# Odd mixer of a two-layer hybrid trunk on one core: the place of the column tiles among the S5 states, and the engine of each convolution chunk

## The chip, the cores and the metric

The kernel runs on one core of a Trainium2 chip. A core has four engines that compute, each with its own queue of instructions: TensorE (PE in the profile; PEld is its loading of weights), VectorE (DVE), ScalarE (ACT) and GpSimd (POOL). SyncE (SP) issues the DMA transfers of this kernel. The metric is the device time of one execution in microseconds; lower is better. Three runs of the kernel before took 1369.16, 1368.41 and 1371.1 us.

## The reference, cut to what matters

The trunk has two layers; each is a mixer and a gated ConvFFN with residual adds. The change lies in the mixer of the second (odd) layer, with a sequence of 512, a model width of 1024 and 512 channels in each of the two branches:

```python
def odd_mixer(h, w_in, conf_dw_w, conf_dw_b, conf_ln_g, conf_ln_b, s5_a_re, s5_a_im,
              s5_b_re, s5_b_im, s5_c_re, s5_c_im, s5_d, s5_log_step, s5_glu_w, w_out):
    proj = h @ w_in
    ca, cg, u = split_cols(proj, [CONF_DIM, CONF_DIM, S5_DIM])
    c = ca * jax.nn.sigmoid(cg)
    c = causal_dwconv(c, conf_dw_w, conf_dw_b)
    c = jax.nn.silu(layer_norm(c, conf_ln_g, conf_ln_b)).astype(F32)
    s = jax.nn.gelu(s5_ssm(u, s5_a_re, s5_a_im, s5_b_re, s5_b_im, s5_c_re, s5_c_im, s5_d, s5_log_step))
    s = s * jax.nn.sigmoid(s @ s5_glu_w.astype(F32))
    mix = jnp.concatenate([c, s], axis=-1).astype(h.dtype)
    return mix @ w_out
```

The depthwise convolution has 31 taps. The S5 part is a complex diagonal recurrence for 32 groups of 16 channels with 64 states each.

## The kernel before, in words

Activations lie transposed: the channels on the 128 partitions, the 512 steps along the free dimension, eight tiles for the model width. A product with a weight is made in three matmuls of 128x512 (lines L100, L101, L102), since weights and activations are split into a high part `hi` and a rest `lo` in a shorter format: hi x hi, hi x lo and lo x hi. A weight tile is loaded by SP into `wraw` (four buffers), cast to `whi` by ACT (L90) and its rest `wlo` made by DVE (L91); `whi` and `wlo` have three buffers each. One column tile of an input product is 8 x 3 = 24 matmuls.

The odd mixer works in four column tiles of 128 channels for each of three products. `glu_in(i)` makes the two products `pca` and `pcg` of the convolution's tile i, multiplies both by the norm's row `R` on DVE, and gates one with the sigmoid of the other. `s5_state(q)` makes the product `pu` of S5 tile q, its multiple `uf` (DVE), regroups it by transposes on PE with copies on ACT between them (`pu2`, `u2`, `puT`, `us`), makes the drive `pS` on PE, and then runs the states on DVE: rotations, two scans (L928, L929) and more rotations into `sst`. `s5_y` makes the outputs `pY` from `us` and `sst` with the matrices `toep` and `w2`, `s5_split` transposes them back (`pyT`), applies GELU and splits the result into `sh` and `slo` for the gate product `pgl`. The output product `po` comes last, and the layer norm of the convolution's result lies beside it. In the profile's names the copies of `u2` show as `u` and the tiles `pu2` as `pu`.

The four chunks of the convolution are made on three engines. For the chunks in `PECONV` (2 and 3) the gated tile is written twice, the second time shifted by a step (`cx`; DVE writes one half, ACT copies the other), and `conv_pe` makes 32 matmuls of 64 output partitions with diagonal weights `kd`, two taps in each. Chunk 0 is in `POOLTAPS`: its 30 taps behind the first run on GpSimd, two instructions each (L858, L859). Chunk 1 has its 30 taps on DVE (L869).

The order of instructions on each engine is fixed when the program is built. The order in the source gives the priority; a `with issue_after(x)` adds that the instructions in it stand behind x on the same engine, with no wait in it. Most tiles of 128x512 come from one pool of 56 slots, and a DMA that fills a slot waits until its last reader is done. PSUM has two sets of four buffers, `pp` for products and `ps` for the rest.

Of the kernel before, what the change touches and what calls it, by code (L numbers as in the profile page):

```python
# [13 lines left out]
ALU = mybir.AluOpType  # L14

P = 128
T = 512
# [6 lines left out]
RH = 4  # L24
SH = 16
NPAIR = SH // 2
POOLTAPS = {0: range(1, 31)}
PECONV = (2, 3)
WV0 = (0, 1, 3, 6)
PACK0 = (("g_mix0", KC),)  # L30
PACK1 = (("ident", P), ("tri", P), ("cw", 48), ("cb", 12), ("dtb", SH), ("alog", SH), ("dsk", NPAIR),
# [5 lines left out]
class Trunk:  # L37
# [774 lines left out]
    def odd(self, st):  # L812
        nc = self.nc
# [4 lines left out]
        mm = nc.tensor.matmul  # L818
        V = nc.vector.tensor_tensor
        cin, cv = [None] * 4, [None] * 4  # L820
        def glu_in(i):
            pa = self.pp("pca")
            self.proj(pa, ins["wca"][i], xs)
            pg = self.pp("pcg")
            self.proj(pg, ins["wcg"][i], xs)
            if "R" not in st:
                self.norm_end(st)
            R = st["R"]
            if i in PECONV:
                a = self.tmp("ca")  # L830
            else:
                a = self.tp.tile([P, T], F32, name="cp", tag="cp", bufs=2) if i in POOLTAPS else self.slot("ca")
            b = self.tmp("cg")
            V(a, pa, R, op=ALU.mult)
            V(b, pg, R, op=ALU.mult)
            nc.scalar.activation(b, b, AF.Sigmoid)
            if i in PECONV:

                x2 = [self.slot("cx") for _ in range(2)]
                for g in range(2):  # L840
                    own, oth = slice(64 * g, 64 * g + 64), slice(64 - 64 * g, 128 - 64 * g)
                    V(x2[g][own], a[own], b[own], op=ALU.mult)
                    nc.vector.memset(x2[g][oth, 0:1], 0.0)
                    nc.scalar.copy(x2[g][oth, 1:], x2[g][own, :T - 1])
                cin[i] = x2
                return
            V(a, a, b, op=ALU.mult)
            cin[i] = a
            o = self.slot(f"cv{i}")
            nc.scalar.activation(o, a, AF.Identity, scale=kw[:, i, 30:31], bias=kb[:, i:i + 1])  # L850
            cv[i] = o
            pa = o
            if i in POOLTAPS and len(POOLTAPS[i]) < 30:
                pa = self.slot("cvp")
                nc.gpsimd.memset(pa, 0.0)
            for s in POOLTAPS.get(i, ()):
                t = self.tp.tile([P, T], F32, name="prod", tag="prod", bufs=1)
                nc.gpsimd.tensor_scalar(t, a, kw[:, i, 30 - s:31 - s], 1.0, op0=ALU.mult, op1=ALU.mult)  # L858
                nc.gpsimd.tensor_tensor(pa[:, s:], pa[:, s:], t[:, :T - s], op=ALU.add)  # L859
            cvp[i] = pa  # L860
# [11 lines left out]
        def conv_loads(i):  # L872
            for h in range(4):
                t = self.slot("kd")
                ld(t, ins["kd"][PECONV.index(i), :, h * T:(h + 1) * T])
                kd.setdefault(i, []).append(t)

        def conv_pe(i):

            p = self.ps("pcv")  # L880
            for j in range(16):
                s = 2 * j
                for g in range(2):
                    w = kd[i][j // 4][:, (j % 4) * P + 64 * g:(j % 4) * P + 64 * g + 64]
                    mm(p[64 * g:64 * g + 64, s:], lhsT=w, rhs=cin[i][g][:, :T - s], start=j == 0, stop=j == 15)  # L885
            cv[i] = cvp[i] = self.slot(f"cv{i}")
            nc.scalar.activation(cv[i], p, AF.Identity, bias=kb[:, i:i + 1])

        us, sst, kd = {}, {}, {}

        def s5_state(q):
            p = self.pp("pu")
            self.proj(p, ins["wu"][q], xs)
            if "R" not in st:
                self.norm_end(st)
            uf = self.slot("uf")
            V(uf, p, st["R"], op=ALU.mult)
            u2 = [self.slot("u2")[:64].rearrange("p (g x) -> p g x", g=4) for _ in range(2)]
            for b in range(2):
                p = self.ps("pu2")  # L900
                for j in range(4):
                    nc.tensor.transpose(p[:64, j * P:(j + 1) * P], uf[:, 4 * b + j::8], self.ident)
                for e in range(2):
                    nc.scalar.copy(u2[e].rearrange("p g (j c) -> p j g c", c=16)[:, 4 * b:4 * b + 4],
                                   p[:64].rearrange("p (j g c) -> p j g c", j=4, g=8)[:, :, 4 * e:4 * e + 4])
            p = self.ps("puT")
            for g in range(8):
                nc.tensor.transpose(p[:, g * 64:g * 64 + 64], u2[g // 4][:, g % 4, :], self.ident[:64, :64])
            u = self.slot("us")
            nc.scalar.copy(u, p)  # L910
            us[q] = u
            w1, rot = s5w[q]
            co, si, rho = rot[:, 0, :], rot[:, 1, :], s5rho[q // 2][:, 256 * (q % 2):256 * (q % 2) + 256]
            p = self.ps("pS")
            for ri in range(2):
                for g in range(8):
                    a = 256 * ri + 64 * (g // 2)
                    mm(p[64 * (g % 2):64 * (g % 2) + 64, a:a + 64], lhsT=w1[ri][:, g * 64:g * 64 + 64],
                       rhs=u[:, g * 64:g * 64 + 64], start=True, stop=True)
            pr, pi = p[:, :256], p[:, 256:]  # L920
            t = [self.tmp("s5rot", 256) for _ in range(4)]
            V(t[0], pr, co, op=ALU.mult)
            V(t[1], pi, si, op=ALU.mult)
            V(t[0], t[0], t[1], op=ALU.add)
            V(t[2], pi, co, op=ALU.mult)
            V(t[3], pr, si, op=ALU.mult)
            V(t[2], t[2], t[3], op=ALU.subtract)
            nc.vector.tensor_tensor_scan(t[1], rho, t[0], 0.0, op0=ALU.mult, op1=ALU.add)  # L928
            nc.vector.tensor_tensor_scan(t[3], rho, t[2], 0.0, op0=ALU.mult, op1=ALU.add)  # L929
            t0, t2 = t[0], t[2]  # L930
            t4, t5 = self.tmp("s5rot", 256), self.tmp("s5rot", 256)
            V(t0, t[1], co, op=ALU.mult)
            V(t2, t[3], si, op=ALU.mult)
            V(t4, t[3], co, op=ALU.mult)
            V(t5, t[1], si, op=ALU.mult)
            s_ = self.slot("sst")
            sv = s_.rearrange("p (a g k) -> p a g k", a=4, g=2)
            nc.vector.memset(sv[:, :, :, 0], 0.0)
            kv = lambda x, g2: x[64 * g2:64 * g2 + 64].rearrange("p (a k) -> p a k", k=64)[:, :, :63]
            for g2 in range(2):  # L940
                V(sv[0:64, :, g2, 1:], kv(t0, g2), kv(t2, g2), op=ALU.subtract)
                V(sv[64:128, :, g2, 1:], kv(t4, g2), kv(t5, g2), op=ALU.add)
            sst[q] = s_

        ss = [None] * 4

# [31 lines left out]
        s5w, s5rho, outw, y2 = {}, {}, {}, {}  # L978
        sx, ev = [None] * 4, [None] * 4

        def s5_loads(q):
            w1 = [self.slot("w1") for _ in range(2)]
            for ri in range(2):
                ld(w1[ri], self.w1d[ri, q])
            rot = self.slot("rot").rearrange("p (r x) -> p r x", r=2)
            ld(rot, self.rotd[0:2, q // 2, :, 256 * (q % 2):256 * (q % 2) + 256].rearrange("r p x -> p r x"))
            s5w[q] = (w1, rot)
            if q % 2 == 0:
                rho = self.slot("rho")
                ld(rho, self.rotd[2, q // 2])  # L990
                s5rho[q // 2] = rho
# [9 lines left out]
        def s5_split(q):  # L1001
            s5_gelu(q, y2[q])
            hi, lo = self.slot("sh", F32R), self.slot("slo", F32R)
            ev[q] = self.split(ss[q], hi, lo)
            sx[q] = (hi, lo)

        glu_in(0)
        s5_loads(0)
        s5_loads(1)
        s5_state(0)  # L1010
        glu_in(1)
        s5_state(1)
        s5_loads(2)
        s5_loads(3)
        s5_state(2)
        s5_state(3)
        for i in PECONV:
            conv_loads(i)
        glu_in(2)
        for q in range(4):  # L1020
            out_loads(q)
        glu_in(3)
        conv_pe(2)
        y2[0] = s5_y(0)
        for q in range(1, 4):
            y2[q] = s5_y(q)
            s5_split(q - 1)
        s5_split(3)
        conv_pe(3)
        conv(1)  # L1030
        mix = [None] * 8
        for m in range(4):
            p = self.pp("pgl")
# [17 lines left out]
        with self.tc.issue_after(self.mark.ins):  # L1051
            for i in (2, 3, 0, 1):
                for t in range(NT):
                    s = slice(i * P, (i + 1) * P)
# [20 lines left out]
        for i in range(4):  # L1075
            p = self.ps("pLNT")
# [8 lines left out]
        for c in range(KC):  # L1085
            p = self.pp("po")
# [112 lines left out]
```

## Time and profile before

| what | value |
|---|---|
| median of three runs | 1369.16 us |
| the profiled execution | 1369.16 us, of which its span 1367.4 us |
| mean granted clock of PE | 0.994 |
| odd mixer, first input product to first output product | 792 to 944 us of the span |
| PE busy in this stretch | 134.36 of 152 us |
| DVE busy in this stretch | 109.26 of 152 us |
| GpSimd busy in this stretch | 69.80 of 152 us |

A row of the profile names the source line, the engine, the operation, what it writes and reads with the buffers' numbers left out, and times in us from the span's start. A wait is put down to the instruction that ended it. The granted clock is the share of its full clock that PE was given.

### The profile page before, as it was taken

The page shows a single profiled execution, that of the slowest core. Times are in us where ns is not written, and L with a number is a line of the kernel's source. Part 1 is how long each engine was busy: PE and PEld are TensorE (multiplying, and loading weights), DVE is VectorE, ACT ScalarE, POOL GpSimd, SP SyncE. Part 2 cuts the span into 40 slices and gives each one's busy share as a digit, 9 for nine tenths or more (in the row PEclk, how much of TensorE's full clock was granted, in tenths as well). Part 3 has the DMA queues.
Part 4 walks back from the last instruction along what each step waited for, and adds up shares of the span by engine and source line. Part 5 has one row for each costly group of instructions (what it writes and reads, how often), then busy time and mean ns, then how long its engine had stood idle before and what let it go on. Part 6 is the DMA issues. An engine that isn't in the chain of part 4 may idle for free.

```text
span 1367.4 us, 17342 instructions
## 1 busy us (share of the span) xinstructions
PE 1326.8 (97%) x6596; PEld 1089.9 (80%) x6596; DVE 941.1 (69%) x1542; ACT 550.0 (40%) x773; POOL 225.3 (16%) x343
## 2 busy tenths in 40 slices
PE   8999999999999999999999997889999999999997
PEld 7788888888887777888888885656888888888887
DVE  6887877679568999877633348974777777774233
ACT  5454544444343443444422222153644444442221
POOL 0210010001206234950000019900000000000100
PEclk9999999999999999999999999999999999999999
DMA  6542233232234334543333343241433333333321
GB/s 223 156 123 70 70 108 108 75 104 70 86 126 129 107 121 117 176 143 97 96 94 103 91 142 103 78 147 41 127 114 98 93 95 105 93 89 97 100 70 63
DMA packets 49957, 145.11 MB, mean 106 GB/s; under 512 B 6481, under 2 KB 7809, under 8 KB 49873
## 3 DMA queue, kind: packets, MB, share of 16 engines
q1 hardware_dynamic: 43712, 126.44, 29.9%
q0 software_dynamic: 5872, 17.37, 4.4%
q8 instruction: 52, 0.85, 0.3%
q14 instruction: 33, 0.26, 0.1%
q10 hardware_dynamic: 288, 0.19, 0.0%
HBM read 133.98 MB, written 9.99 MB: 105 GB/s over the span
## 4 chain that ended last, share of the span: by engine, by line
PE 81%; DVE 14%; issue 2%; ACT 2%; DMA 1%; POOL 0%; SPq 0%; DVEq 0%; ACTq 0%; POOLq 0%
PE pup L102 9%; PE pup L100 9%; PE pup L101 9%; PE pdn L101 6%; PE pdn L102 6%; PE pdn L100 6%; DVE ffa L190 3%; PE po L100 3%; PE po L102 3%; PE po L101 3%; DVE wlo L91 2%; PE pcv L885 2%; PE pxbc L101 1%; PE pxbc L100 1%; PE pxbc L102 1%
## 5 line engine op out<-in xcount | busy, mean ns | idle before, releaser
L90 ACT CAST whi<-wraw 128x1024 fp32r<-128x1024 f32 (+3 forms) x246 | 230.9, 939 | 461.1 <-PE pdn L101 135.0
L91 DVE TENSOR_TENSOR wlo<-wraw,whi 128x1024 fp32r<-128x1024 f32 (+3 forms) x246 | 270.3, 1099 | 157.4 <-ACT whi L90 157.0
L102 PE MATMUL pup<-xh,wlo 128*128 128x512 f32 x704 | 274.6, 390 | 3.6 <-DVE wlo L91 3.6
L100 PE MATMUL pup<-xh,whi 128*128 128x512 f32 x704 | 275.0, 391 | 2.5 <-ACT whi L90 2.5
L101 PE MATMUL pup<-xl,whi 128*128 128x512 f32 x704 | 273.9, 389 | 0.0
L102 PEld LDWEIGHTS pup<-xh,wlo 128*128 128x128 f32 x704 | 132.1, 188 | 33.3 <-DVE wlo L91 5.7
L190 DVE SCALAR_TENSOR_TENSOR ffa<-ffh,c,ffa 128x511 f32<-128x511 f32 (+1 forms) x176 | 155.7, 885 | 3.2 <-ACT ffa L187 0.3
L100 PEld LDWEIGHTS pup<-xh,whi 128*128 128x128 f32 x704 | 132.2, 188 | 30.2 <-ACT whi L90 3.4
L101 PEld LDWEIGHTS pup<-xl,whi 128*128 128x128 f32 x704 | 132.2, 188 | 27.3
L100 PE MATMUL pdn<-acth,whi 128*128 128x512 f32 (+1 forms) x374 | 140.9, 377 | 0.0
L101 PE MATMUL pdn<-actl,whi 128*128 128x512 f32 (+1 forms) x374 | 140.8, 377 | 0.0
L102 PE MATMUL pdn<-acth,wlo 128*128 128x512 f32 (+1 forms) x374 | 140.8, 377 | 0.0
L185 DVE TENSOR_TENSOR ffh<-pup,R 128x512 f32<-128x512 f32 x88 | 60.4, 686 | 57.0 <-PE pup L102 56.8
L187 ACT ACTIVATE ffa<-ffh,c 128x512 f32<-128x512 f32 x88 | 71.9, 817 | 50.0 <-DVE ffh L185 46.9
L232 POOL TENSOR_SCALAR x<-x,c 128x512 f32<-128x512 f32 (+1 forms) x9 | 9.1, 1016 | 459.6 <-ACT acc L128 360.2
L100 PEld LDWEIGHTS pdn<-acth,whi 128*128 128x128 f32 x374 | 70.4, 188 | 12.9
L101 PEld LDWEIGHTS pdn<-actl,whi 128*128 128x128 f32 x374 | 70.4, 188 | 12.9
L102 PEld LDWEIGHTS pdn<-acth,wlo 128*128 128x128 f32 x374 | 70.4, 188 | 12.8
L100 PE MATMUL po<-mh,whi 128*128 128x512 f32 x192 | 75.2, 393 | 0.7 <-ACT mh L95 0.7
L102 PE MATMUL po<-mh,wlo 128*128 128x512 f32 x192 | 75.5, 393 | 0.0
L101 PE MATMUL po<-ml,whi 128*128 128x512 f32 x192 | 75.5, 393 | 0.0
L95 ACT CAST acth<-ffg 128x512 fp32r<-128x512 f32 x44 | 27.3, 621 | 115.8 <-DVE ffg L197 111.2
(421 smaller groups left out, 2294.2 us busy)
## 6 DMA issues: line engine op xcount, KB each, us to landing
wraw<-in_wup_dram SPq DMA_DIRECT2D x88, 512.0 KB, 3.6
wraw<-in_wdn_dram SPq DMA_DIRECT2D x32, 512.0 KB, 3.6
wraw<-in_weo_dram SPq DMA_DIRECT2D x32, 256.0 KB, 3.0
wraw<-in_wxbc_dram SPq DMA_DIRECT2D x12, 512.0 KB, 3.6
wraw<-in_wdn_dram SPq DMA_DIRECT2D x16, 384.0 KB, 3.1
wraw<-in_wz_dram SPq DMA_DIRECT2D x8, 512.0 KB, 3.7
wraw<-in_wg_dram SPq DMA_DIRECT2D x8, 512.0 KB, 3.7
ar<-acd POOLq DMA_DIRECT2D x16, 256.0 KB, 3.9
```

What stands on the lines that cost most here:

```text
L90: nc.scalar.copy(hi[:, :n], raw[:, :n])
L91: (eng or nc.vector).tensor_tensor(lo[:, :n], raw[:, :n], hi[:, :n].bitcast(F32), op=ALU.subtract)
L95: self.nc.scalar.copy(hi, src)
L100: mm(out, lhsT=w[0], rhs=x[0], start=start, stop=False)
L101: mm(out, lhsT=w[0], rhs=x[1], start=False, stop=False)
L102: self.mark = mm(out, lhsT=w[1], rhs=x[0], start=False, stop=stop)
L185: nc.vector.tensor_tensor(h, p, st["R"], op=ALU.mult)
L187: nc.scalar.activation(a, h, AF.Identity, scale=dw[:, j, 2:3], bias=db[:, j:j + 1])
L190: nc.vector.scalar_tensor_tensor(a[:, s:], h[:, :T - s], dw[:, j, tap:tap + 1], a[:, s:], op0=ALU.mult, op1=ALU.add)
L232: self.nc.gpsimd.tensor_scalar(self.x[c][:, ts], self.x[c][:, ts], st["g"][:, c:c + 1], 1.0, op0=ALU.mult, op1=ALU.mult)
L885: mm(p[64 * g:64 * g + 64, s:], lhsT=w, rhs=cin[i][g][:, :T - s], start=j == 0, stop=j == 15)
```

## The change

Chunk 1 of the convolution goes from DVE to PE, chunk 0 from GpSimd to DVE, and GpSimd has no part of the mixer any more. `s5_state` is cut in two: `s5_in(q)` makes `pu` and `uf`, and `s5_state(q)` starts at the transposes, which are put behind the last matmul that was written before it (`mark`). Between `s5_in(q)` and `s5_state(q)` now stands `glu_in(q + 1)`, and `conv_pe(1)` before the last state. The three blocks of `conv_pe` are spread between the states and the outputs, each with its own `conv_loads`, and `conv(0)` on DVE is put behind the last state.

```diff
-POOLTAPS = {0: range(1, 31)}
-PECONV = (2, 3)
+POOLTAPS = {}
+PECONV = (1, 2, 3)
@@
                 for g in range(2):
                     w = kd[i][j // 4][:, (j % 4) * P + 64 * g:(j % 4) * P + 64 * g + 64]
-                    mm(p[64 * g:64 * g + 64, s:], lhsT=w, rhs=cin[i][g][:, :T - s], start=j == 0, stop=j == 15)
+                    self.mark = mm(p[64 * g:64 * g + 64, s:], lhsT=w, rhs=cin[i][g][:, :T - s], start=j == 0, stop=j == 15)
@@
-        def s5_state(q):
+        ufs = {}
+
+        def s5_in(q):
             p = self.pp("pu")
             self.proj(p, ins["wu"][q], xs)
             if "R" not in st:
                 self.norm_end(st)
-            uf = self.slot("uf")
-            V(uf, p, st["R"], op=ALU.mult)
+            ufs[q] = self.slot("uf")
+            V(ufs[q], p, st["R"], op=ALU.mult)
+
+        def s5_state(q):
+            uf, mark = ufs[q], self.mark
             u2 = [self.slot("u2")[:64].rearrange("p (g x) -> p g x", g=4) for _ in range(2)]
             for b in range(2):
                 p = self.ps("pu2")
-                for j in range(4):
-                    nc.tensor.transpose(p[:64, j * P:(j + 1) * P], uf[:, 4 * b + j::8], self.ident)
+                with self.tc.issue_after(mark.ins):
+                    for j in range(4):
+                        nc.tensor.transpose(p[:64, j * P:(j + 1) * P], uf[:, 4 * b + j::8], self.ident)
@@
-                V(sv[64:128, :, g2, 1:], kv(t4, g2), kv(t5, g2), op=ALU.add)
+                last = V(sv[64:128, :, g2, 1:], kv(t4, g2), kv(t5, g2), op=ALU.add)
             sst[q] = s_
+            return last
@@
         glu_in(0)
         s5_loads(0)
         s5_loads(1)
+        s5_in(0)
+        glu_in(1)
         s5_state(0)
-        glu_in(1)
-        s5_state(1)
+        s5_in(1)
         s5_loads(2)
         s5_loads(3)
+        glu_in(2)
+        s5_state(1)
+        s5_in(2)
+        conv_loads(1)
+        glu_in(3)
         s5_state(2)
-        s5_state(3)
-        for i in PECONV:
-            conv_loads(i)
-        glu_in(2)
+        s5_in(3)
+        conv_pe(1)
+        states = s5_state(3)
+        conv_loads(2)
         for q in range(4):
             out_loads(q)
-        glu_in(3)
+        y2[0] = s5_y(0)
+        y2[1] = s5_y(1)
+        s5_split(0)
         conv_pe(2)
-        y2[0] = s5_y(0)
-        for q in range(1, 4):
-            y2[q] = s5_y(q)
-            s5_split(q - 1)
+        conv_loads(3)
+        y2[2] = s5_y(2)
+        s5_split(1)
+        y2[3] = s5_y(3)
+        s5_split(2)
+        conv_pe(3)
         s5_split(3)
-        conv_pe(3)
-        conv(1)
+        conv(0, after=states)
```

Three places show how the built order moves. The first is TensorE's queue around the transposes of S5 state 1. Before, they stand inside the `pu` product of the next tile (L902 is `pu2`, L908 is `puT`):

```order
L101 MATMUL pu<-xl,whi 128x512
L902 MATMUL pu_7298<-c_106,uf 64x128 x4
L902 MATMUL pu_7305<-c_106,uf 64x128 x4
L102 MATMUL pu<-xh,wlo 128x512
L100 MATMUL pu<-xh,whi 128x512
```

Now the last matmul of `pcg` of tile 2 stands ahead of them, and the next `pu` behind them (L908 is `pu2` here):

```order
L101 MATMUL pcg<-xl,whi 128x512
L102 MATMUL pcg<-xh,wlo 128x512
L908 MATMUL pu_7302<-c_106,uf 64x128 x4
L908 MATMUL pu_7309<-c_106,uf 64x128 x4
L100 MATMUL pu<-xh,whi 128x512
```

Between the `pu` that makes `uf` and the transposes that read it now stand 48 product matmuls, and 17 more stand between these transposes and `puT`.

The second place is VectorE's queue at the states. Before, the `uf` of tile 1 and the first taps of chunk 1 (L869) stand behind the whole of state 0, whose last instruction is L942:

```order
L942 TENSOR_TENSOR sst<-s5rot 64x4x63
L835 TENSOR_TENSOR cg<-pcg,R 128x512
L91 TENSOR_TENSOR wlo<-wraw,whi 128x1024
L847 TENSOR_TENSOR ca<-ca,cg 128x512
L897 TENSOR_TENSOR uf<-pu,R 128x512
L869 SCALAR_TENSOR_TENSOR cv_7261<-ca,c_447,cv_7261 128x511
L869 SCALAR_TENSOR_TENSOR cv_7261<-ca,c_447,cv_7261 128x510
```

Now the `uf` of the next tile (L899) stands behind the second scan of a state (L935):

```order
L934 SCALAR_TENSOR_TENSOR s5rot<-rho,s5rot 128x256
L933 TENSOR_TENSOR s5rot<-s5rot 128x256
L938 TENSOR_TENSOR s5rot<-s5rot,rot 128x256
L935 SCALAR_TENSOR_TENSOR s5rot<-rho,s5rot 128x256
L899 TENSOR_TENSOR uf<-pu,R 128x512
L939 TENSOR_TENSOR s5rot<-s5rot,rot 128x256
```

The 30 taps, now of chunk 0, all stand behind the last instruction of state 3 (L948), with one `slo` among them and three behind them.

The third place is ScalarE's queue between the `pu2` and `puT` transposes of a state (`u` is `u2` here). Before, the four copies of `u2` follow each other:

```order
L904 COPY u_7296<-pu_7298 64x4x4x16
L904 COPY u_7297<-pu_7298 64x4x4x16
L904 COPY u_7296<-pu_7305 64x4x4x16
L904 COPY u_7297<-pu_7305 64x4x4x16
L90 CAST whi<-wraw 128x1024
L910 COPY us<-puT 128x512
```

Now the two shifted copies of `cx` of the tile just made stand between the first and the second of them:

```order
L836 ACTIVATE cg<-cg 128x512
L910 COPY u_7484<-pu_7486 64x4x4x16
L844 COPY cx<-cx 64x511 x2
L910 COPY u_7485<-pu_7486 64x4x4x16
L910 COPY u_7484<-pu_7493 64x4x4x16
L910 COPY u_7485<-pu_7493 64x4x4x16
L916 COPY us<-puT 128x512
```

Three of the four `u2` copies so come behind an operation that waits for VectorE. On SP's queue the loads `kd` of chunk 1 now stand behind the third `wgl` load, those of chunk 2 behind the third `woo` load and ahead of the sixteen `toep` and `w2` loads, and those of chunk 3 behind these. On GpSimd's queue 60 instructions are gone.

## The prediction

> **What bounds the kernel now.** I read the page first, for the balance of the whole.
>
> ```profile
> span 1367.4 us, 17342 instructions
> PE 1326.8 (97%) x6596; PEld 1089.9 (80%) x6596; DVE 941.1 (69%) x1542; ACT 550.0 (40%) x773; POOL 225.3 (16%) x343
> PE 81%; DVE 14%; issue 2%; ACT 2%; DMA 1%; POOL 0%; SPq 0%; DVEq 0%; ACTq 0%; POOLq 0%
> ```
>
> TensorE (PE) is busy for 97% of the span, so time is won only where PE idles or runs slowly, and every matmul added costs its length. The chain that ended last still holds 14% VectorE (DVE). The stretches of the odd mixer say where. Columns: length of the stretch, busy time of each engine with its instructions, granted PE clock, share of the DMA engines, GB/s.
>
> ```profile
> 810.35:819.88 9.53, 9.53 (x43) 7.83 (x42) 4.58 (x7) 4.81 (x5) 5.25 (x5) 1.00 0.65 215
> 819.88:824.39 4.51, 4.51 (x57) 3.52 (x55) 0.32 (x1) 2.81 (x6) 4.06 (x6) 1.00 0.51 187
> 824.39:840.38 15.99, 10.04 (x47) 8.02 (x44) 15.76 (x21) 2.40 (x3) 14.90 (x13) 0.92 0.15 37
> 840.38:854.59 14.21, 11.18 (x75) 8.39 (x76) 13.97 (x18) 4.00 (x8) 13.30 (x11) 0.85 0.49 162
> 854.59:863.26 8.67, 6.67 (x58) 4.99 (x58) 8.58 (x11) 1.85 (x5) 7.94 (x9) 0.80 0.01 2
> 880.85:892.37 11.52, 5.93 (x25) 4.24 (x24) 11.35 (x16) 1.25 (x2) 8.03 (x7) 1.00 0.08 24
> 892.37:907.43 15.06, 15.06 (x65) 6.84 (x67) 14.49 (x25) 3.62 (x6) 0.00 (x0) 0.89 0.94 330
> 907.43:912.02 4.59, 4.59 (x76) 4.34 (x72) 4.38 (x7) 2.50 (x7) 0.00 (x0) 1.00 0.01 4
> 912.02:914.56 2.54, 2.54 (x42) 2.30 (x40) 0.74 (x2) 2.50 (x5) 0.00 (x0) 1.00 0.00 0
> 920.91:934.39 13.48, 13.48 (x66) 4.51 (x64) 1.39 (x2) 2.51 (x4) 0.00 (x0) 1.00 0.00 1
> 934.39:943.60 9.21, 9.21 (x43) 7.62 (x41) 5.10 (x9) 6.97 (x11) 0.00 (x0) 1.00 0.21 61
> ```
>
> From 824 to 892 DVE is full (8.58 of 8.67, 13.97 of 14.21) while PE idles 5.95, 3.03, 2.00 and 5.59 us in four of these rows. The waits of PE between 803 and 944 name what it waits for (total, times, longest):
>
> ```profile
> PE pu L902 <- DVE uf L897: 11.0, 3, 5.9
> PE pcv L885 <- ACT cx L844: 4.2, 1, 4.2
> PE pcg L102 <- DVE wlo L91: 1.4, 1, 1.4
> ```
>
> All three lead to DVE: `uf`, `cx` and `wlo` stand behind state chains and convolution taps. And DVE is slow there. The trace's groups of DVE and of GpSimd (POOL), as minimum/median/maximum ns with first and last start, or as busy us and mean ns:
>
> ```profile
> L859 POOL TENSOR_TENSOR cv<-cv,prod x30: 1075/1287/2317, 815.0 to 888.3; 128x511 f32<-128x511 f32 x1, 128x510 f32<-128x510 f32 x1, 128x509 f32<-128x509 f32 x1, 128x508 f32<-128x508 f32 x1
> L941 DVE TENSOR_TENSOR sst<-s5rot x8: 403/1358/1482, 832.5 to 886.3; 64x252 f32<-64x252 f32 x8
> L869 DVE SCALAR_TENSOR_TENSOR cv<-ca,c,cv 128x510 f32<-128x510 f32 x1 | 1.1, 1060 | 0.0
> L869 DVE SCALAR_TENSOR_TENSOR cv<-ca,c,cv x22: 721/730/742, 889.7 to 911.3; 128x504 f32<-128x504 f32 x1, 128x503 f32<-128x503 f32 x1, 128x502 f32<-128x502 f32 x1, 128x501 f32<-128x501 f32 x1
> L928 DVE TENSOR_TENSOR_SCAN s5rot<-rho,s5rot 128x256 f32<-128x256 f32 x4 | 3.4, 840 | 0.0
> L929 DVE TENSOR_TENSOR_SCAN s5rot<-rho,s5rot 128x256 f32<-128x256 f32 x4 | 4.4, 1093 | 0.0
> ```
>
> While POOL runs its 30 taps (815 to 888) the same DVE shape takes 403 to 1482 ns and a tap 1060; after 889 a tap takes 730. Last, each long idle slows PE. Two-microsecond stretches of PE (length, busy, clock):
>
> ```profile
> 838.00:840.00 2.00, 0.00 (x0) 0.50 0.00 0
> 840.00:842.00 2.00, 1.62 (x9) 0.50 0.99 290
> 842.00:844.00 2.00, 2.00 (x10) 0.50 0.93 274
> 856.00:858.00 2.00, 2.00 (x7) 0.50 0.00 0
> 862.00:864.00 2.00, 0.74 (x7) 1.00 0.16 31
> ```
>
> After the idles of 5.95 and 3.03 us the clock stands at 0.50; after the idle of 2.00 us, which ended at 863.26, it stays at 1.00. So these rows lose 16.6 us to idling and some 5 us to the clock: 1.6 in the 892.37 row (15.06 us against 13.48 for as many matmuls), 2 over 840 to 846, 1.5 over 855 to 859.
>
> **The change, part by part.** Everything before 810.35 and behind 943.60 (where the output product begins) keeps its rows, so I sum the new stretch from 810.35, as PE sees it, against 133.25 us.
>
> *Products.* Nine of 24 matmuls (`pca`, `pcg`, `pu`), nothing added: 9.53 us for 42 gives 0.227 each, 216 x 0.227 = 49.0.
>
> *States 0 to 2.* The rows on TensorE show the transposes of state q behind `glu_in(q+1)` and inside the next `pu`. The stretch 819.88 to 824.39 holds one state with seven product matmuls: 4.51 - 7 x 0.227 = 2.92 each, 8.76 in all. The wait for `uf` goes: its multiply now stands behind the second scan of the state before, and 24 `pca` and 24 `pcg` matmuls (10.9 us) lie between that state and its reader. A state is 15 DVE operations of about 0.41 us and two scans, 0.84 and 1.09: 8 us at most without POOL. What is late next is `puT`: in ScalarE's (ACT) order its copies `u2` now stand behind the two `cx` copies.
>
> ```profile
> 820.52 1.18 ACT L904 COPY u<-pu 64x256 f32<-64x256 f32 x4 [3.65 <-PE pu L902]
> 891.70 1.34 ACT L844 COPY cx<-cx 64x511 f32<-64x511 f32 x2 [1.22 <-DVE cx L842]
> 904.35 0.68 DVE L842 TENSOR_TENSOR cx<-ca,cg 64x512 f32<-64x512 f32 x1
> 816.89 1.29 DVE L91 TENSOR_TENSOR wlo<-wraw,whi 128x1024 fp32r<-128x1024 f32 x1 [2.85 <-ACT whi L90]
> 822.99 1.05 ACT L90 CAST whi<-wraw 128x1024 fp32r<-128x1024 f32 x1
> ```
>
> After `pcg` ends: cast 1.05, `wlo` 1.29, `cx` 0.68 on DVE, `cx` copies 1.34, two `u2` copies 0.59: 5.0 with the queues' gaps. PE arrives 0.8 (transposes) + 17 x 0.227 = 4.65 later. I take 0.4 a state, 1.2 in all; the bounds are 0 and, with the slow DVE durations, about 5.5 us (the third rival).
>
> *Convolution.* `conv_pe(1)` is a third block of 13.48 us on the path: 3 x 13.48 = 40.4. Its weights `kd` stand in SP's queue behind the third `wgl` load, which waits for the last `pcg`'s `wlo` (made about 843); they leave at 845 and are needed at 869. The 30 taps of chunk 0 on DVE (30 x 0.73, about 23 us with gaps, from about 895) lie beside the second and third blocks; the chunk is read behind the first output products, after 940. Three of four `slo` stand behind these taps until 919 and the gate product reads them from 925 on: that cover is 5 us or more, and nothing is paid. On POOL 60 instructions go, none follows them, nobody waits.
>
> *State 3* stands alone behind `conv_pe(1)`: no product covers its copies, so 4.51, about 2 us of it idle in two pieces.
>
> *S5 outputs.* Two `pY` with one `pyT` 4.59, two times `pY` and `pyT` 2.54, a last `pyT` 0.5: 10.2. The loads `kd`(2) and `toep`/`w2` wait in SP's queue behind a `woo` load that waits for the third `wgl`'s `wlo`, behind state 2: issued from about 876.
>
> ```profile
> 862.95 4.10 SPq L875 DMA_DIRECT2D kd<-in_kd_dram  x8
> 891.66 0.33 SPq L997 DMA_DIRECT2D toep<-tpd  x1
> 901.10 0.32 SPq L998 DMA_DIRECT2D w<-w2d  x1
> DMA to landing us min/median/max: 3.0/5.4/6.5
> ```
>
> Sixteen such loads went out in 9.8 us (891.66 to 901.42), 0.6 each. The ninth, which ends what the first `pY` needs, goes out at 881 and lands by 887.5; PE is there at 887.2. I take 0.5; bounds 0 and 5 (1.2 us a load).
>
> *Gate product.* 39 matmuls as in the 934.39 row, 9.21, and nine before them, 2.0. `s5_split(3)` now follows the last block, so PE waits for GELU and split of tile 3: 0.45.
>
> **Sum:** 49.0 + 8.8 + 1.2 + 40.4 + 4.5 + 10.2 + 0.5 + 11.7 = 126.3 against 133.25, 7.0 us less. The profiled execution took 1369.16 us (1.76 around its span), which is also the median of the three runs; so 1362.2.
>
> [...]
>
> **The rivals.**
> 1. *The loads come late.* For: one SP queue, 21 loads behind one wait. Against: 0.6 us each in this trace. At 1.2 us each the first `pY` waits 5 instead of 0.5: 1366.7. Chance 12%.
> 2. *Half clock behind state 3.* A drop lasted about 4 us (840 to 845), so 4 us of work take 2 more: 1364.2. Chance 8%.
> 3. *Slower than before: `puT` waits.* DVE may keep its slow durations without POOL:
>
> ```profile
> 825.21 0.42 DVE L922 TENSOR_TENSOR s5rot<-pS,rot 128x256 f32<-128x256 f32 x1
> 836.20 0.82 DVE L942 TENSOR_TENSOR sst<-s5rot 64x252 f32<-64x252 f32 x1
> 860.53 1.97 DVE L91 TENSOR_TENSOR wlo<-wraw,whi 128x1024 fp32r<-128x1024 f32 x1
> ```
>
> A state of 11.8 us (825.21 to 837.02), `uf`, `ca` and two `wlo` of 1.97 then end 17.1 us after `pS`; `pcg` ends 11.6 us after it, so `cg`, `cx` and behind them `u2` are 5.5 us late in states 1 and 2, each followed by 2 us lost to half clock (15 us). Taps of 1.06 us behind a slow state 3 hold `slo` about 6 us too long: some 1383. From 3.5 us a state on the gain is gone (2 x 3.5). Against: the 730 ns taps once POOL is still. Chance 5%.
> 4. *The idling moves and eats the gain:* small waits at each change of tile (the product rows already hold some) add 7 us; 1369. Chance 5%.
>
> That the work doesn't move is no rival: the rows show it moved.
>
> **How the numbers follow.** Forecast 70%, own range 1359.0 to 1364.0: its lower end has none of the small waits (1.2 + 0.5 + 0.45) and 1 us less in state 3. The range reaches to 1366.5 for rivals 1 and 2 and leaves out rivals 3 and 4 and the end of 1. A measurement here can tell 0.2% (2.7 us), so faster means under 1366.4: forecast, rival 2 and about two thirds of rival 1, 0.86; same 0.08; slower 0.06.
>
> **What would show it.** Right: PE waits for `uf` and `cx` gone; the three `pcv` blocks at 13.5 us; clock 1.00 from 810 on; state chains of 7 to 8 us; the output product at about 936.5. Wrong: waits of PE for `u2` above 1 us, for `toep` or `kd` above 2, a clock below 1.00, or DVE taps above 0.8 us.

## The result, and the profile after

| | before | after |
|---|---|---|
| median of four runs | 1369.3 us (1368.41 to 1371.1) | 1360.3 us (1358.76 to 1361.88) |
| ratio | | 0.9929, 95% interval 0.9917 to 0.9941 |
| the profiled execution | 1369.16 us, span 1367.4 | 1361.88 us, span 1360.1 |
| mean granted clock of PE | 0.994 | 0.999 |

The forecast was 1362.2 us. The stretch that it summed, from the first `pca` of tile 1 to the first `po`, is now read from the same view of stretches; `po` begins at 936.62. (Columns as before: length, busy time of PE, PEld, DVE, ACT and POOL with their instructions, clock, share of the DMA engines, GB/s.)

```profile
812.41:870.84 58.43, 58.43 (x362) 47.18 (x360) 34.52 (x72) 21.69 (x37) 0.00 (x0) 1.00 0.42 136
870.84:884.32 13.48, 13.48 (x65) 4.51 (x65) 6.01 (x15) 0.54 (x1) 0.00 (x0) 1.00 0.42 136
884.32:888.37 4.05, 2.80 (x50) 2.41 (x50) 0.00 (x0) 2.32 (x6) 0.00 (x0) 1.00 1.05 386
888.37:892.62 4.25, 4.25 (x79) 4.01 (x75) 4.00 (x11) 1.81 (x6) 0.00 (x0) 1.00 1.05 390
892.62:906.00 13.38, 13.38 (x66) 4.68 (x66) 12.78 (x22) 3.76 (x6) 0.00 (x0) 1.00 0.31 115
906.00:911.03 5.03, 5.03 (x83) 4.55 (x79) 4.85 (x8) 3.69 (x8) 0.00 (x0) 1.00 0.00 0
911.03:924.51 13.48, 13.48 (x66) 4.53 (x64) 8.44 (x12) 2.92 (x7) 0.00 (x0) 1.00 0.01 1
924.51:925.15 0.64, 0.64 (x10) 0.57 (x8) 0.00 (x0) 0.52 (x1) 0.00 (x0) 1.00 0.00 0
925.15:936.62 11.47, 11.31 (x50) 9.04 (x49) 6.11 (x10) 8.34 (x13) 0.00 (x0) 1.00 0.15 46
```

The rows are: the products with states 0 to 2, the first `pcv` block (the matmuls of `conv_pe` for one chunk), state 3, the first outputs, the second block, more outputs, the third block, the last `pyT`, the gate product. PE is busy in all of every row but the third and, by 0.16 us, the last, and the clock stands at 1.00 in all of them. PE's idle time in the stretch fell from 17.3 to 1.4 us. Its busy time rose from 115.9 to 122.8, by 6.9 only, although a block of 13.48 came in: the rest of its work takes 6.6 us less than before, when the mean clock of the stretch was 0.95.

The rows add to 124.2 us against 133.25 before: 9.0 us less. That is also the difference of the medians. The profiled pair differs by 7.3 us only, because everything ahead of the stretch took 2.06 us longer in the profiled execution of after (812.41 against 810.35), where the change has nothing.

PE's waits between 803 and 944 (total, times, longest) are now these, in place of 11.0 us for `uf`, 4.2 for `cx` and 1.4 for `wlo`:

```profile
PE pS L924 <- ACT us L916: 0.7, 1, 0.7
PE puT L914 <- ACT u L910: 0.6, 1, 0.6
PE prow L147 <- DVE rs_y L121: 0.3, 1, 0.3
PE pgl L101 <- DVE slo L96: 0.2, 1, 0.2
```

And DVE has become fast. The groups of the same operations (minimum/median/maximum ns, first and last start):

```profile
L947 DVE TENSOR_TENSOR sst<-s5rot x8: 405/412/417, 836.2 to 894.1; 64x252 f32<-64x252 f32 x8
...
L934 DVE TENSOR_TENSOR_SCAN s5rot<-rho,s5rot x4: 679/681/681, 832.8 to 890.3; 128x256 f32<-128x256 f32 x4
...
L935 DVE TENSOR_TENSOR_SCAN s5rot<-rho,s5rot x4: 679/682/685, 834.1 to 891.5; 128x256 f32<-128x256 f32 x4
```

The convolution's taps in DVE's timeline (start, length, and how many follow each other):

```profile
895.00 13.19 DVE L869 SCALAR_TENSOR_TENSOR cv<-ca,c,cv 128x511 f32<-128x511 f32 x17
...
908.71 9.88 DVE L869 SCALAR_TENSOR_TENSOR cv<-ca,c,cv 128x494 f32<-128x494 f32 x13
```

The first of the two `sst` lines (L941 before, L947 now) had a median of 1358 ns and went from 403 to 1482; now all eight lie between 405 and 417. The scans went from 840 and 1093 ns to 681 and 682. A tap takes 13.19 / 17 = 0.78 us.

### The profile page after: what moved, and what is told of

Read it like the earlier page. It is cut to its first block, busy times and chain, and to the rows that moved or that the text cites. A ratio compares the mean times of both kernels' runs of the same rounds, so it can differ in the third digit from the quotient of the medians.

```text
span 1360.1 us, 17410 instructions
## 1 busy us (share of the span) xinstructions
PE 1335.5 (98%) x6660; PEld 1092.1 (80%) x6660; DVE 918.6 (68%) x1545; ACT 550.7 (40%) x775; POOL 155.6 (11%) x283
## 4 chain that ended last, share of the span: by engine, by line
PE 86%; DVE 10%; issue 2%; ACT 1%; DMA 1%; POOL 0%; DVEq 0%; SPq 0%; ACTq 0%; POOLq 0%
PE pup L102 9%; PE pup L100 9%; PE pup L101 9%; PE pdn L102 6%; PE pdn L100 6%; PE pdn L101 6%; DVE ffa L190 3%; PE po L100 3%; PE pcv L885 3%; PE po L102 3%; PE po L101 3%; DVE wlo L91 2%; PE pxbc L101 1%; PE pxbc L100 1%; PE pxbc L102 1%
## 5 line engine op out<-in xcount | busy, mean ns | idle before, releaser
L102 PEld LDWEIGHTS pdn<-acth,wlo 128*128 128x128 f32 x374 | 70.4, 188 | 12.9
```

The lines of the kernel that those rows point to most:

```text
L102: self.mark = mm(out, lhsT=w[1], rhs=x[0], start=False, stop=stop)
```

## The experiments

The change does two things at once: it takes GpSimd out and gives its work away, and it reorders products and states. The theory was the prediction's: GpSimd's taps slowed DVE, and `uf`, `cx` and `wlo` stood in a slow queue. The rivals were that the order alone, or the engines alone, are the gain. Ratios are to the kernel before on the same chip. The rows come from four sets of runs in which the kernel before took 1369.3, 1370.04, 1369.32 and 1370.35 us, so a difference of about 1 us between medians of different sets tells nothing.

| kernel | order | GpSimd | chunks on DVE | `pcv` blocks | median us | ratio, 95% interval |
|---|---|---|---|---|---|---|
| before | old | chunk 0 | 1 | 2 | 1369.3 | 1 |
| after | new | none | 1 | 3 | 1360.3 | 0.9929, 0.9917 to 0.9941 |
| old order, new engines | old | none | 1 | 3 | 1361.17 | 0.9940, 0.9925 to 0.9955 |
| new order, old engines | new | chunk 0 | 1 | 2 | 1365.48 | 0.9969, 0.9957 to 0.9980 |
| after with 30 unread pairs | new | unread | 1 | 3 | 1376.87 | 1.0052, 1.0037 to 1.0067 |
| after with 60 scalings | new | unread | 1 | 3 | 1364.57 | 0.9969, 0.9959 to 0.9979 |
| after with 120 short pairs | new | unread | 1 | 3 | 1364.92 | 0.9960, 0.9946 to 0.9974 |
| two chunks on DVE, taps last | new | none | 2 | 2 | 1348.13 | 0.9842, 0.9828 to 0.9857 |
| the same, taps ahead of `pgl` | new | none | 2 | 2 | 1356.02 | 0.9907, 0.9892 to 0.9922 |
| two chunks on DVE, taps last, old order | old | none | 2 | 2 | 1350.12 | 0.9856, 0.9841 to 0.9871 |
| two and a half chunks on DVE | new | none | 2.5 | 1.5 | 1345.40 | 0.9825, 0.9811 to 0.9840 |
| the same, norm later | new | none | 2.5 | 1.5 | 1341.67 | 0.9793, 0.9778 to 0.9808 |

### The order without the engines

Against after (the single block `conv_pe(2)` goes ahead of state 3, `conv_pe(3)` stays):

```diff
-POOLTAPS = {}
-PECONV = (1, 2, 3)
+POOLTAPS = {0: range(1, 31)}
+PECONV = (2, 3)
@@
-        conv(0, after=states)
+        conv(1, after=states)
```

> The new order with the old share of the engines: chunk 0 on GpSimd, chunk 1 on VectorE behind the states, chunks 2 and 3 on TensorE (two pcv blocks instead of three, so 13.5 us of TensorE work less than the changed kernel). Theory (GpSimd's taps slow VectorE's two-input operations, and the new order alone doesn't cover that): state chains of about 11 us as before, uf, cx and u2 late again, puT waits some 4 to 6 us in states 1 and 2, each followed by about 2 us of half clock; 1358 to 1366 us, so 0 to 5 us from the changed kernel in spite of 13.5 us less work. Rival (the order alone is what gains): no waits above 1 us, 1346 to 1349 us.

It took 1365.48 us. PE's waits between 803 and 950:

```profile
PE puT L914 <- ACT u L910: 6.8, 4, 3.0
PE pgl L101 <- DVE slo L96: 4.8, 1, 4.8
PE pu L102 <- DVE wlo L91: 1.6, 2, 0.9
```

With GpSimd beside it the new order doesn't wait for `uf` any more but for `u2`, `wlo` and, since the taps begin behind a later state 3, for `slo`: 13.2 us. So the order alone brings 4.6 us against before on the same chip (1370.04); it exchanges late operands for others.

### The engines without the order

Against before:

```diff
-POOLTAPS = {0: range(1, 31)}
-PECONV = (2, 3)
+POOLTAPS = {}
+PECONV = (1, 2, 3)
@@
+        conv_pe(1)
         conv_pe(2)
@@
-        conv(1)
+        conv(0, after=states)
```

> The old order with the new engines: chunk 0 on VectorE behind the last state, chunks 1 to 3 on TensorE, no GpSimd. Theory (VectorE is fast without GpSimd, so the waits for uf shrink but don't vanish, because uf still stands behind a state chain, and that for cx nearly goes): state chains of 7 us, pu waits 0 to 2 us three times instead of 2 to 6, 13.5 us more TensorE work; 1362 to 1368 us, so 2 to 8 us slower than the changed kernel. Rival A (the order is the whole gain): waits for uf of 11 us stay, 1378 us or more. Rival B (the engines are the whole gain): no waits, within 1 us of the changed kernel.

It took 1361.17 us, 0.9 more than after, with intervals that overlap; each against its own before, it is 8.9 us less and after is 9.0 less. The theory expected 2 to 8 more than after and missed; the time is rival B's, though the waits are not quite gone. The longest waits of PE between 803 and 944:

```profile
PE pu L902 <- DVE uf L897: 1.2, 2, 0.7
PE pyT L972 <- ACT y L965: 0.6, 1, 0.6
```

`uf` still stands behind a whole state chain here, as before. It cost 11.0 us then and costs 1.2 now, because the chain is short: the `sst` of L941 take 405 to 418 ns (median 412) in place of 403 to 1482 (median 1358). The taps have also left the states in this kernel, which could be a reason too; but with two chunks on DVE in the old order (below) they stand among the states again, and `uf` costs 0.3 us. What the reordering was to cover is nearly gone without it.

### GpSimd beside the changed kernel

After, with work on GpSimd that nobody reads, begun where the old taps began:

```diff
+        pt_ = [self.tp.tile([P, T], F32, name=n, tag=n, bufs=1) for n in ("cp", "prod")]
+        nc.gpsimd.memset(pt_[0], 0.0)
+        for s in range(1, 31):
+            nc.gpsimd.tensor_scalar(pt_[1], cin[0], kw[:, 0, 30 - s:31 - s], 1.0, op0=ALU.mult, op1=ALU.mult)
+            nc.gpsimd.tensor_tensor(pt_[0][:, s:], pt_[0][:, s:], pt_[1][:, :T - s], op=ALU.add)
         s5_in(0)
```

> The changed kernel with work added on GpSimd alone: 30 pairs of a scaling and an addition of 128x512 from the time of the first states on, as the old taps of chunk 0 were, whose result nobody reads. Theory (it is GpSimd's access beside VectorE that made VectorE slow): rotations and additions without PSUM go from 0.41 to 1.3 us, scans from 0.68 to 0.84 and 1.09, a state chain from 6.8 to 11 us or more; puT waits 4 to 6 us in states 1 and 2 with about 2 us of half clock behind each; 1370 to 1385 us. Rival (VectorE was slow for another reason, its own taps between the states): chains of 7 us, within 2 us of the changed kernel's time.

It took 1376.87 us, slower than before. The stretch is 142.3 us long (810.43 to 952.74), 18.1 more than after. PE's long idles in its timeline (start, length of the instruction behind it, and in brackets the idle and what ended it):

```profile
827.21 0.73 PE L914 MATMUL puT<-c,u 64*128 64x64 f32 x8 [0.97 <-ACT u L910]
...
845.09 0.50 PE L102 MATMUL pu<-xh,wlo 128*128 128x512 f32 x1 [1.80 <-DVE wlo L91]
...
852.88 1.11 PE L914 MATMUL puT<-c,u 64*128 64x64 f32 x8 [4.09 <-ACT u L910]
...
873.58 0.50 PE L102 MATMUL pu<-xh,wlo 128*128 128x512 f32 x1 [2.41 <-DVE wlo L91]
...
879.31 1.11 PE L914 MATMUL puT<-c,u 64*128 64x64 f32 x8 [2.71 <-ACT u L910]
```

They add to 12.0 us. The clock falls to 0.66, 0.93 and 0.72 in the ten-microsecond stretches from 850, 870 and 880, and PE is busy for 128.8 us instead of 122.8 with the same matmuls, which is the other 6 us. No data hangs on the added work, and the tile that it reads is held for DVE's later taps anyway; so the 16.6 us over after come from GpSimd's being busy. State 2 shows the same within one trace: GpSimd ends at 887.0, the first scan, before that, takes 1.19 us, the second, from 888.1 on, 0.68, and the four `sst` behind it 0.40 to 0.42.

### What of GpSimd's work collides

The two lines of the loop became two scalings, each with one tensor input:

```diff
-            nc.gpsimd.tensor_tensor(pt_[0][:, s:], pt_[0][:, s:], pt_[1][:, :T - s], op=ALU.add)
+            nc.gpsimd.tensor_scalar(pt_[0], cin[0], kw[:, 0, 30 - s:31 - s], 1.0, op0=ALU.mult, op1=ALU.mult)
```

> As the changed kernel with work added on GpSimd alone, but now 60 scalings of 128x512 with one tensor input (no addition with two), result unread. Theory A (any work of GpSimd on SBUF slows VectorE's operations that read two tensors from SBUF): rotations and sst at 0.8 to 1.4 us while it lasts, puT waits as with the pairs; 1368 us or more. Theory B (only GpSimd's own two-tensor additions collide): VectorE's durations stay at 0.41 and 0.68 us, no waits of PE above 1 us, 1359 to 1362 us.

1364.57 us lies between the two theories: beside operations with one input `sst` takes up to 0.82 us too, but they cost less in all, 4.3 us over after in place of 16.6. (They also ended earlier, at 869 instead of 887.) DVE's and then GpSimd's timeline at the end of state 0 (start, length):

```profile
836.39 0.82 DVE L947 TENSOR_TENSOR sst<-s5rot 64x252 f32<-64x252 f32 x1
837.22 0.82 DVE L948 TENSOR_TENSOR sst<-s5rot 64x252 f32<-64x252 f32 x1
838.05 0.82 DVE L947 TENSOR_TENSOR sst<-s5rot 64x252 f32<-64x252 f32 x1
838.88 0.82 DVE L948 TENSOR_TENSOR sst<-s5rot 64x252 f32<-64x252 f32 x1
839.74 0.69 DVE L834 TENSOR_TENSOR ca<-pca,R 128x512 f32<-128x512 f32 x1
```

```profile
836.92 0.85 POOL L1021 TENSOR_SCALAR cp<-ca,c 128x512 f32<-128x512 f32 x1
837.76 0.85 POOL L1020 TENSOR_SCALAR prod<-ca,c 128x512 f32<-128x512 f32 x1
838.59 0.86 POOL L1021 TENSOR_SCALAR cp<-ca,c 128x512 f32<-128x512 f32 x1
839.41 0.86 POOL L1020 TENSOR_SCALAR prod<-ca,c 128x512 f32<-128x512 f32 x1
```

The starts alternate, one period of 0.83 us for both: for DVE the 0.41 that `sst` takes in after, and as much again. `ca`, which reads PSUM and one tensor in SBUF, keeps the 0.69 that it takes in after. To tell turns from a shared rate, the 30 pairs were cut into quarters:

```diff
+            for k in range(4):
+                c = slice(k * P, k * P + P)
+                nc.gpsimd.tensor_scalar(pt_[1][:, c], cin[0][:, c], kw[:, 0, 30 - s:31 - s], 1.0, op0=ALU.mult, op1=ALU.mult)
+                nc.gpsimd.tensor_tensor(pt_[0][:, c], pt_[0][:, c], pt_[1][:, c], op=ALU.add)
```

> The changed kernel with the same added amount of GpSimd work as in the run with 30 pairs (1376.9 us), but cut into quarters: 120 pairs of a scaling and an addition of 128x128, result unread. In that run and with 60 scalings the starts of VectorE's and GpSimd's operations alternate. Theory A (the two take turns by whole instructions, so VectorE's operation with two SBUF inputs waits for the end of GpSimd's): short turns make short waits, sst at 0.5 to 0.75 us instead of 0.82 to 1.4, puT waits of 1 to 2 us in states 1 and 2, 1361 to 1367 us. Theory B (the two share a rate, whatever the length of an instruction): sst again at 0.8 to 1.4 us and the time at 1372 us or more.

It took 1364.92 us, as theory A expected. Busy us and mean ns of `sst` between 818 and 892, in this run and then in the one with whole pairs:

```profile
L947 DVE TENSOR_TENSOR sst<-s5rot 64x252 f32<-64x252 f32 x6 | 3.2, 540 | 0.0
L948 DVE TENSOR_TENSOR sst<-s5rot 64x252 f32<-64x252 f32 x6 | 3.2, 540 | 0.1
```

```profile
L948 DVE TENSOR_TENSOR sst<-s5rot 64x252 f32<-64x252 f32 x6 | 5.8, 962 | 0.1
L947 DVE TENSOR_TENSOR sst<-s5rot 64x252 f32<-64x252 f32 x6 | 4.1, 682 | 0.0
```

The same elements in shorter instructions cost DVE 0.13 us an operation. With whole pairs the means hold, in each line, two of six operations from after GpSimd's end; the other four took 0.82 us (L947) and 1.23 us (L948), which is 0.41 and 0.82 more than alone. That is what turns by whole instructions would give. This run alone doesn't rule out a shared rate, since GpSimd's own work took nearly twice as long (128.5 us busy up to 944 instead of 67.4) and so passed fewer elements in a microsecond; the starts that alternate (period 0.83 us) speak for turns, and no run here shows more than that. (PE still lost 1.9 us to `u2` and 1.2 to `slo`.)

### Is the third block needed?

Once DVE is fast it has room: it was busy in 76.7 of the 124.2 us. Against the kernel with the new order and old engines, chunk 0 goes to DVE too, and both chunks are written behind the gate product, so that every other operation goes first:

```diff
-POOLTAPS = {0: range(1, 31)}
+POOLTAPS = {}
@@
-        conv(1, after=states)
@@
             mix[4 + m] = (hi, lo)
+        conv(0)
+        conv(1)
```

> As the first of these four, with chunk 0 on VectorE too: two chunks (60 taps) on VectorE, written behind the gate product so that they come last in priority and fill VectorE's free places, chunks 2 and 3 on TensorE, none on GpSimd. TensorE has the same work as in the first of these four, 13.5 us less than in the changed kernel. Theory: VectorE at its fast durations has room for the second chunk (30 x 0.76 = 23 us) beside the states and the products; no waits above 1 us but up to 3 us at the gate product, whose slo stand behind all 60 taps; 1346 to 1351 us. Rival (VectorE becomes the bound: taps between the states make u2 late, or the 60 taps hold slo): 1355 us or more.

1348.13 us, 17.4 less than with chunk 0 on GpSimd, with the same matmuls (the taps of chunk 1 are also free to begin before state 3 here). PE's longest waits between 803 and 924 are short:

```profile
PE puT L914 <- ACT u L910: 1.2, 3, 0.6
PE pS L924 <- ACT us L916: 0.7, 1, 0.7
```

So the change gave back most of a block, 12.2 us (12.9 with each against its own before), for taps that DVE can carry. The same engines in the old order show what the reordering is worth then:

> The old order of products and states with chunks 0 and 1 on VectorE (taps written last), chunks 2 and 3 on TensorE, none on GpSimd. Against the same engines in the new order (1348.1 us) it shows what the order is worth. Theory (freeing VectorE of GpSimd carried the change; the order is worth about 1 us, as with three chunks on TensorE): uf waits of up to 1 us each, 1348.5 to 1351 us. Rival (with 60 taps VectorE is full again and uf, behind state chains and taps, is late by several us as before; the order is worth 5 us or more): 1353 us or more.

1350.12 us (1346.79 to 1350.28), as the theory expected, and 2.0 more than in the new order (2.7 with each against its own before). The intervals overlap, and one of its runs is below all of the other's, so this doesn't settle whether the order is worth anything here. Taps stand among the states on DVE in this kernel, as they did before, and `uf` still costs next to nothing without GpSimd:

```profile
PE pu L902 <- DVE uf L897: 0.3, 1, 0.3
```

Where the taps are written matters more. With `conv(0)` and `conv(1)` ahead of the gate product:

> As the kernel with both chunks on VectorE and taps written last (1348.1 us), with one edit: the two chunks are written ahead of the gate product, so their taps outrank the gate product's wlo, of which the third then stands behind some 12 taps; the loads woo, kd and toep/w2 queued behind it on SyncE leave some 10 us later. Theory (the first rival of the prediction, late loads, is a real cost where that wait comes late): pY waits for toep 4 to 6 us, with up to 2 us of half clock behind it; 1352 to 1356 us. Rival (the loads have more slack than their issue times say): no wait above 1 us, 1347.5 to 1349 us.

1356.02 us, 7.9 more (8.6 with each against its own before). The loads of `toep` leave SP from 885.51 on instead of 877.89, and PE waits:

```profile
PE pY L965 <- DMA toep<-tpd: 5.0, 2, 4.4
```

That is the prediction's first rival, late loads, made real by a `wlo` behind taps: 5 us of waiting, and half clock (0.50) from 889 to 897, during it and behind it.

### Taking more from TensorE

Of chunk 3, 16 taps stay on PE and 15 go to DVE. The lines below leave out that DVE writes the plain tile for these taps, that half of the block's weights are loaded, and that the layer norm's transposes now take chunk 3 last:

```diff
-            for j in range(16):
+            nj = 8 if i == 3 else 16
+            for j in range(nj):
@@
         conv(0)
         conv(1)
+        cin[3] = plain3[0]
+        conv(3, range(16, 31))
```

> As the kernel with both chunks on VectorE and taps written last (1348.1 us), with half of chunk 3 taken from TensorE: 16 of its taps in a pcv block of half the length, the other 15 on VectorE in the time that stood free there behind the second split (11 us idle before the fourth slo, 1 us gaps behind it). VectorE writes the plain tile once more (0.68 us). Theory (TensorE's own work is what is left): 6.7 us less, 1341 to 1343 us. Rival (the 15 taps, 11 us, end too late for the transposes of the layer norm): 1344 us or more, with waits of PE for cv or for zs.

1345.40 us: 2.7 of the 6.7 us arrived, and the theory's range was missed. The two profiled executions, 1348.36 and 1344.11 us, are 4.3 apart, which is 6.7 less this one new wait of PE:

```profile
PE po L102 <- DVE wlo L91: 2.2, 1, 2.2
```

That `wlo` stood behind the layer norm's statistics, and these behind the last tap. So the norm was put two columns later:

```diff
-        out_s5(range(2))
+        out_s5(range(4))
@@
-        out_s5(range(2, KC))
+        out_s5(range(4, KC))
```

> The fastest kernel so far (half of chunk 3's taps on VectorE, 1345.4 us) with one edit: four instead of two columns of the output product are written ahead of the layer norm's transposes and statistics, so that the wlo of the third column, for which TensorE waited 2.2 us, no longer stands behind the statistics on VectorE. Theory (that wait is what was lost): 1342.5 to 1344 us. Rival (the norm's chain becomes late for pLNT, or the wait moves to another wlo): 1345 us or more.

1341.67 us, 28.7 below before on the same chip (1370.35) and the fastest of the study; that wait is gone. The profiled executions of the two kernels, 1344.11 and 1341.94 us, differ by 2.2, as that wait does. The medians differ by 3.7, more than the theory expected, and nothing here shows where the rest comes from.

## Why the prediction was right

Point by point, in the order of its sum:

- **Products and states 0 to 2**, 59.0 with the waits for `u2`: 58.43. The term of 1.2 us for `u2` is 0, since the two waits listed lie in state 3; the matmuls took 0.6 more than the 57.8 worked out for them. The scans' 0.68 rather than 0.84 and 1.09 had no part in that: ahead of states 1 and 2 DVE stood idle for 1.87 and 2.29 us before `cg`, waiting for `pcg`. In state 1 the transposes took 1.0 us instead of 0.8, so PE reached `puT` 4.86 us after `pcg` instead of 4.65, and the copies that it needed were done.
- **Convolution**, 40.4: 13.48, 13.38 and 13.48, together 40.3. The taps lie beside the blocks, and `pgl` waits 0.2 us for `slo`.
- **State 3**, 4.5: 4.05, with 1.25 us idle in two pieces of 0.6 and 0.7 instead of 2. Both are there as forecast, only shorter.
- **Outputs and their loads**, 10.2 and 0.5: 4.25 + 5.03 + 0.64 = 9.9 and no wait. The ninth of the loads left SP at 881.34, where 881 was worked out, and it landed in time.
- **Gate product**, 11.7: 11.47, with 0.16 us idle where 0.45 had been put for the wait.

So 126.3 us were forecast and 124.2 came, and the time is 1.9 us under the forecast, inside its own range. Against the sum, the waits for `u2`, loads and state 3 came out 1.2, 0.5 and 0.45 us smaller, 2.15 in all: each small wait put in as a caution was too large. The other terms nearly cancel, with 0.6 us more for the products and 0.6 less for outputs, gate product and convolution. That `po` begins at 936.62, where about 936.5 was named as a sign, is luck: the stretch began 2.06 us late in this execution and was 2.1 us shorter than forecast.

One reason was attributed too narrowly. The prediction let the wait for `uf` go because its multiply was moved ahead and other products stand between. The old order with the new engines shows that 9.8 of these 11.0 us go without the move: the chain in front of `uf` got short. Moving matters only where the chain is long, and there (new order, old engines) it exchanges the wait for `uf` against one for `u2`. What carried the change is the sentence about DVE's durations beside POOL.

The rivals: **late loads** didn't occur, though the run with taps ahead of the gate product shows 5.0 us of waiting and a clock of 0.50 from 889 to 897 where a `wlo` slips. **Half clock behind state 3** didn't occur, and neither did **idling that moves**: the waits between 803 and 944 add to 1.8 us. The clock rows of after around its two idles (length, busy, clock):

```profile
884.00:886.00 2.00, 1.42 (x11) 1.00 1.06 400
886.00:888.00 2.00, 1.32 (x28) 1.00 1.07 383
888.00:890.00 2.00, 2.00 (x50) 1.00 1.03 387
```

The clock stayed at 1.00 around these idles of 0.6 and 0.7 us. **`puT` waits** was right in its mechanism and its place, as the run with 30 pairs shows: 5.9 us (1.80 for a `wlo` and 4.09 for `u2`) and 5.1 us (2.41 + 2.71) in states 1 and 2, where 5.5 were worked out for `u2` alone. It was wrong in the condition, since DVE did not stay slow without POOL. Its price of 1383 was too high against 1376.87, because `slo` was late by 0.2 us and not by 6: GpSimd had ended at 887, before the taps.

## What to carry to other kernels

Where an engine is slow, look for who works beside it before its queue is reordered: the same shape at 403 and at 1482 ns in one trace said more than any wait, and the new share of the engines brought in the old order nearly all that the whole change brought (8.9 of 9.0 us). Work taken from a neighbour should first be tried on the engine that has just become fast, written last so that it fills gaps; the block that went to TensorE cost some 12 us here. And an operation that feeds a load queue (`wlo`, on which SP waits) must not stand behind filler: with the taps ahead of the gate product PE waited 5.0 us for `toep`.

## What was not expected of the hardware

Beside 60 scalings, for which GpSimd reads one tensor only, the starts of `sst`, which reads two in SBUF, and of the scalings alternate at the end of state 0, with a period of 0.83 us against 0.41 for `sst` alone. DVE's operations with an operand in PSUM keep their time beside the 30 pairs: four lines of `s5rot` from `pS` (128x256) take 0.41 to 0.42 us and `ca` and `cg` (128x512) 0.69, as in after.

In these runs the length of an idle alone does not tell what becomes of PE's clock. In the old order with two chunks on DVE an idle of 1.6 us for `slo` was followed by a clock of 0.50; in the kernel with two and a half chunks it stayed at 1.00 behind one of 2.2 us for `wlo`. First the one, then the other, as length, busy and clock:

```profile
895.00:897.00 2.00, 0.79 (x9) 1.00 0.00 0
897.00:899.00 2.00, 1.66 (x10) 0.76 0.00 0
899.00:901.00 2.00, 2.00 (x6) 0.50 0.00 0
```

```profile
928.00:930.00 2.00, 0.20 (x2) 1.00 0.00 0
930.00:932.00 2.00, 1.58 (x7) 1.00 0.26 84
932.00:934.00 2.00, 2.00 (x11) 1.00 0.78 261
```

What does decide it was not tried, and stays open.
